# Odd weights' differences for gates, queries and keys made in the odd stage, and five units of output weights loaded inside the branch

## The chip, the cores and the metric

The kernel runs on one core of one Trainium2 chip. The metric is the device time of one execution in microseconds (us); lower is better. The engines are named as in the profile: PE (TensorE, matmuls), PEld (its weight loads), DVE (VectorE), ACT (ScalarE), POOL (GpSimd) and SP (SyncE, which only issues transfers here). POOL and ACT issue transfers too. Every engine works through its own list of instructions in the order that was fixed when the program was compiled.

## The reference, cut to what matters

A decoder of two layers, for one prompt of 2048 rows and for 64 sample rows (8 sequences of 8), model width 1024, all in float32.

```python
# layer 0 (even): pooling mixer and differential attention behind one projection
pu, pg, q, k, v, ag = split(x @ w_in_even)          # 1024 -> 3072
a   = softmax(q1 k1) - lam * softmax(q2 k2)         # 4 heads, causal
mix = concat([pool(pu) * silu(pg), rms_norm(a @ v) * silu(ag)])
y   = layer_norm(alpha * x + mix @ w_out_even)
# layer 1 (odd): gated linear attention, 4 heads, key 128, value 256
q, k, v, g = split(y @ w_in_odd)                    # 1024 -> 3072
log_a = log_sigmoid((y @ w_ga) @ w_gb + b_g) / 16
o, state = gla(q, k, v, log_a, state0)              # chunked scan
out = layer_norm(alpha * y + (rms_norm(o) * silu(g)) @ w_out_odd)
```

## The kernel before, in words

**Products.** A float32 product is made of three passes over a high and a low part (lines 51 to 53: high by high, low by high, high by low). Whatever PE multiplies is therefore split first: a copy that rounds to the high part (line 40 on ACT, 42 on POOL, 44 on DVE) and a subtraction for the low part (line 45). Weights come in units of 512 KB: a load by SP into one of two raw tiles (`wr`, line 375), then the split into one of four places.

**Fast products.** Both input projections are cut into groups of 1024 output columns: 0, 1, 2. For most groups the halves of rows, inner dimension and columns make a 2 by 2 block product, which `fast` computes with seven products instead of eight. It needs sums of the input's blocks (`s1` to `s4`) and, for each group, four differences of the weights' quarters (`t1` to `t4`). The class `WParts` makes those differences and keeps them in DRAM, in one of two ways:

- `make` works on pieces of 128 by 256: four loads, four subtractions (lines 301 to 304), four stores, all transfers issued by POOL (lines 351 and 353). One set of four tiles (pool `comb`) serves all pieces, eight pieces to a group.
- `make_wide` works on pieces of 4 by 128 by 512: one load (line 335; the first two of a call are issued by ACT, the others by POOL), the same four subtractions at twice the width, four stores by POOL (line 339). Two tiles take turns, four pieces to a group.

**Order of the even stage.** `project_even` runs groups 0, 1, 2 for the first 1024 rows and then for the second. Its local `run` advances a generator `parts` by one piece every so many steps. `parts` makes the even weights' own differences (groups 1 and 2 wide, group 0 narrow; tiles `pn` and `pmb`), and then the odd weights' differences for all three groups, narrow, in the order 1, 2, 0. In the profile these last are the tiles `rmb` and the DRAM tensor `rt`. `comb` is closed when the projection ends, and the pools that attention opens next take over that memory: among them `arp`, with the tiles `oq` (attention's results), `sga` (gates) and `sq`.

**Attention.** Heads 0 to 3, each over 16 blocks of 128 rows, `t` from 0. A block has scores (`sc`, lines 1016 and 1017), exponentials (`e`, line 1036), the difference of the two softmaxes (line 1045), transposes (`tp`, line 1068), products with the values (`po`, line 1061, one PSUM bank) and the copy of `po` into `oq` (line 1088, ACT). `weave` deals out filling work beside it by estimated cost: beside head 0 the first half of the output projection (`out_pool`, tiles `zp` on PE, `zh` and `zl` on POOL, 17 blocks of rows); beside head 1 the sample's attention (`Sample`, tiles `sk`, `ssc` and others), whose pool opens when `out_pool`'s memory is free; beside heads 2 and 3 the second half of the output projection with the norm.

**Order of the odd stage.** `project_odd` runs, for the first 1024 rows, group 0 with all eight products (`plain_rows`, which needs no differences), then group 1 and group 2 with `fast`; for the second 1024 rows groups 0, 1 and 2 with `fast`. Its local `run` advances a second generator beside the products: gates and the sums `s1` to `s4` of the input's blocks (`X.sums`). `s4` is used by the last of the seven products of `fast`.

**The branch.** After the projection the kernel loads the units `k` of the odd output weights (`w1_out`, eight in all, unit 0 earlier), reads one flag into a register and takes one of two branches, each of which runs the chunked scan `Gla.run`. Inside, `fill(i)` computes chunk `i` (`mix`: tiles `go` and `gsp`, state `S`), and `out(i)` multiplies its result by the eight units (`gz`). Nothing is moved across the branch.

The scheduler that fixes each engine's order simulates the program at compile time; the order in which the code states the work is its priority, so a piece stated early can run late.

Of the kernel before, what the change touches and what calls it, by code (L numbers as in the profile page):

```python
# [12 lines left out]
F32 = mybir.dt.float32  # L13
# [68 lines left out]
def places(wp):  # L82
    def f(i):
        return tuple(wp.tile([128, 1024], F32R, tag=f"w{z}", name=f"w{z}{i}") for z in "hl")
    return f
# [98 lines left out]
def fast(nc, X, w, fm, bank, qbank, room, sink, order=ORDER, scale=lambda j: 1.0, side=None):  # L184

    ps, t = {}, {}

    def open_(m, j):  # L190
        c = FIRST.get(m)
        if c:
            ps[c, j] = (qbank if c == "q" else bank)(f"f{m}_{j}")

    def mul(m, j, wm, k):
        p, a = ps[CHAIN[m], j], PARTS[m][0]
        js = slice(128 * j, 128 * j + 128)
        xs = [(lambda _, z=z: z[a][:, k, :] if fm else z[a][:, k, js]) for z in (X.hi, X.lo)]
        ws = [(lambda _, z=z: wm[z](k)[:, js] if fm else wm[z](k)) for z in range(2)]
        l, r = (ws, xs) if fm else (xs, ws)  # L200
        mm3(nc, p, *l, *r, 1, first=(m in FIRST and k == 0), last=(k == 3), skip_group_check=True)

    def done(m, j):
        p = ps[CHAIN[m], j]
        if m in (1, 6, 7):
            t[m, j] = room({1: "t", 6: "u", 7: "v"}[m], j)
            nc.scalar.activation(t[m, j], p, AF.Copy, scale=scale(j) if m == 1 else 1.0)
        elif m == 4:
            sink("21", j, p)
        else:  # L210
            o = t[{2: 1, 5: 7, 3: 6}[m], j]
            if m == 2 and scale(j) != 1.0:
                nc.vector.scalar_tensor_tensor(out=o, in0=p, scalar=scale(j), in1=o, op0=ALU.mult, op1=ALU.add)
            else:
                nc.vector.tensor_tensor(out=o, in0=p, in1=o, op=ALU.add)
            sink({2: "11", 5: "22", 3: "12"}[m], j, o)

    for m in order:
        wm = w(PARTS[m][1])
        if side:  # L220
            side(m, wm, True)
        for j in range(4):
            open_(m, j)
        for u in (0, 2):
            for j in range(4):
                for k in (u, u + 1):
                    mul(m, j, wm, k)
                if u:
                    done(m, j)
                    yield m, j  # L230
        if side:
            side(m, wm, False)
# [232 lines left out]
def project_even(tc, d, P, P2, W, slot, psf):  # L465


    nc = tc.nc
    xr, banks = ExitStack(), ExitStack()
    with ExitStack() as own:  # L470
# [72 lines left out]
        def all_parts():  # L543
            yield from P.make_wide(wide, (1, 2), X.last)
            yield from P.make(comb, (0,))

            P2.last = P.last
            yield from P2.make(comb, (1, 2, 0))

        parts = all_parts()  # L550

# [761 lines left out]
class Odd:  # L1313
# [34 lines left out]
    def run(self):  # L1348
        tc, d, ctx = self.tc, self.d, self.ctx
        nc = tc.nc  # L1350
        self.steep = self.pool(ctx, "p1s", 1).tile([1, 32], I32, name="steep")[:, 0:1]
        cst = self.pool(self.p1, "p1c", 1)
        tu = self.pool(self.p1, "p1t", 4)
        last = project_odd(tc, d, self, cst, tu)
        early = None
        for m, j in last:
            if (m, j) == (7, 3):

                self.xq.close()
                G = Gla(tc, d, self.ident, self.raw, self.pool(ctx, "gl", 1, side="right"))  # L1360
                early = self.early(G, self.pool(ctx, "gw0", 1, side="right"))
            elif early:
                next(early, None)
        for _ in early:
            pass
        self.p1.close()
        self.fill_banks.close()
        gw = places(self.pool(ctx, "gw", 3, side="right"))
        for k in range(1, 8):
            self.out_weights(G, k, gw if k > 4 else self.place)  # L1370
        G.buf["s"] = [self.raw.tile([128, 1024], F32, tag="raw", name=f"gs_{i}") for i in range(2)]
        r = nc.values_load(self.steep[0:1, 0:1], min_val=0, max_val=1)
        with tc.If(r < 1) as c:
            G.run(True)
        with c.Else():
            weights_inside(tc, d)
            G.run(False)
# [23 lines left out]
def plain_rows(X, nc, w, bank, sink):  # L1401

    for f in "12":
        wm = {i: w("b" + i + f) for i in "12"}
        for z in "12":
            ps = {}
            for i in "12":
                a = "a" + z + i
                for u in (0, 2):
                    for j in range(4):  # L1410
                        js = slice(128 * j, 128 * j + 128)
                        if j not in ps:
                            ps[j] = bank(f"f{z}{f}_{j}")
                        for k in (u, u + 1):
                            mm3(nc, ps[j], lambda _: wm[i][0](k)[:, js], lambda _: wm[i][1](k)[:, js],
                                lambda _: X.hi[a][:, k, :], lambda _: X.lo[a][:, k, :], 1,
                                first=(i == "1" and k == 0), last=(i == "2" and k == 3), skip_group_check=True)
                        if i == "2" and u:
                            sink(z + f, j, ps[j])
                        if j % 2:  # L1420
                            yield


def project_odd(tc, d, O, cst, tu):
# [92 lines left out]
    def queries_keys(h, given):  # L1517

        def sink(which, j, ap):
            t0 = 1024 * h + 512 * (which[0] == "2")  # L1520
            q = which[1] == "1"
            if not given or which == "21":
                e = slot(f"qe{h}{which}_{j}")
                nc.scalar.activation(e, ap, AF.Copy, scale=128 ** -0.5 if q else 1.0)
                ap = e
            nc.gpsimd.dma_start(d["q1" if q else "k1"][j, :, t0:t0 + 512], ap)
        return sink

    def values(h):
        def sink(which, j, ap):  # L1530
            t0 = 1024 * h + 512 * (which[0] == "2") + 128 * j
            if which == "21":
                e = slot(f"ve{h}_{j}")
                nc.scalar.activation(e, ap, AF.Copy)
                ap = e
            nc.gpsimd.dma_start(d["v1"][t0:t0 + 128, 512 * (which[1] == "2"):][:, :512], ap)
        return sink
# [40 lines left out]
            return cst.tile([128, 512], F32, tag="se", name=n)  # L1578
        return SampleSide(nc, x_s, qbank, place_, slot, done, name)

    def run(gen, then=(), wait=4):

        then = iter(then)
        for i, _ in enumerate(gen):
            if later:
                later.pop(0)()
            if i >= wait:
                next(then, None)

    def weights(g):  # L1590
        return P.loader(W, g)
# [5 lines left out]
    def first_parts():  # L1597
        yield from islice(sums, 8)
        ga, _ = gate_weights(0, False)
        for z in "12":  # L1600
            yield from gates(f"0{z}", 512 * (z == "2"), 512,
                             [t for i in "12" for k in range(4) for t in both(f"a{z}{i}", ga, k, 4 * (i == "2"))])

        yield from ("",) * 2
        for x in islice(sums, 4):
            yield x
# [1 line left out]
    def first_weights(x):  # L1608
        return O.first.pop(x) if x in O.first else weights(0)(x)

    run(plain_rows(X, nc, first_weights, bank, queries_keys(0, False)), first_parts(), wait=8)
    O.few.close()
    O.ev = O.pool(O.p1, "p1e", 8)
    run(fast(nc, X, weights(1), False, bank, qbank, place, values(0)), sums)
    nw = norm_weights(0)

    def next_parts():
# [84 lines left out]
class Gla:  # L1702
# [103 lines left out]
    def run_in(self, ctx, fast):  # L1806
# [31 lines left out]
        def prepare(i):  # L1838
            r = R[i]
            if i > 1:  # L1840
                yield from self.inside(i, 1, fast, bank)
            if i:
                self.split_v = self.two("v", r, "v1", "act")
            if i or not fast:
                self.two("a", r, "att", "dve")
            if i:
                r["qs"] = tuple(wk.tile([128, 4, 128], F32R, tag=f"q{z}", name=f"gq{z}{i}") for z in "hl")
                split(nc, r["q"], *r["qs"], "act")
# [173 lines left out]
        def fill(i):  # L2022
            yield from mix(i)
            if i:
                scale(i)
            else:

                yield from prepare(1)
                with tc.issue_after(self.split_v[0].ins), tc.issue_after(self.split_v[1].ins):
                    scale(0)  # L2030
            for _ in range(3):
                x = next(side, None)
                if x is not None:
                    yield x
            if 0 < i < 15:
                yield from prepare(i + 1)
            if i < 14:
                load(i + 2, first + ("v1",))
# [360 lines left out]
```

## Time and profile before

| | |
|---|---|
| three runs | 2235.43, 2237.23 and 3998.26 us, median 2237.23 |
| profiled execution | 2234.13 us, of which the span 2232.3 us |
| granted PE clock, mean | 0.962 of full speed |
| PE busy | 2042.4 us, 91% of the span, 10769 matmuls |
| DVE, ACT, POOL busy | 1525.8, 976.7 and 918.9 us |
| bytes moved | 405.67 MB, mean 182 GB/s |

The profile is of one execution and all its times are in us from the span's start, unless marked ns. "Busy" leaves out the issuing of transfers on SP, but for POOL the transfers' issue is counted. A row of waits reads: engine, tile, line, what ended the wait, total, times, longest. A row of the timeline reads: start, duration, engine, line, operation, written tile from read tile, shape, count, and in brackets the idle time just before it with what ended it. A row of stretches reads: start and end, length, busy time with the number of instructions in brackets for each engine, granted PE clock, share of the DMA engines, GB/s.

### The profile page before, as it was taken

How to read it: one execution, taken by the hardware profiler on the slowest of the kernel's cores; microseconds unless marked ns; L12 is line 12 of the kernel's file. 1: busy time of each engine (PE TensorE's matmuls, PEld its weight loads, DVE VectorE, ACT ScalarE, POOL GpSimd, SP SyncE). 2: the span in 40 equal slices, each digit the busy share in tenths (PEclk: the TensorE clock that was granted, in tenths of full speed). 3: DMA queues.
4: the chain of work that ended last, by engine and by line, in shares of the span. 5: the costliest groups of instructions: out<-in, count | busy, mean ns of one | idle time of the engine just before them, and what ended most of it. 6: DMA issues, size and time to landing. Idle time of an engine off the chain costs nothing. (4 is left out here: it accounts for less than half of the span.)

```text
span 2232.3 us, 31671 instructions
## 1 busy us (share of the span) xinstructions
PE 2042.4 (91%) x10769; PEld 1658.7 (74%) x10769; DVE 1525.8 (68%) x2905; ACT 976.7 (44%) x1809; POOL 918.9 (41%) x1257
## 2 busy tenths in 40 slices
PE   8999998989689999779888989999999896999987
PEld 7778786867557677667777768888887675877876
DVE  7697757757735676688676756736734558789994
ACT  4244342435302565465555533535527653333341
POOL 2445535346576334277463321122211122465654
PEclk9999999998899999899998999999999997999999
DMA  8877877469876778343232243456643457445522
GB/s 294 276 235 249 280 235 233 147 165 279 262 265 200 230 244 258 119 119 116 93 119 68 86 144 114 165 199 202 200 149 114 160 175 245 147 160 185 164 100 73
DMA packets 211294, 405.67 MB, mean 182 GB/s; under 512 B 30530, under 2 KB 107714, under 8 KB 211122
## 3 DMA queue, kind: packets, MB, share of 16 engines
q1 hardware_dynamic: 139490, 231.43, 34.2%
q0 software_dynamic: 52192, 160.59, 20.3%
q10 hardware_dynamic: 19440, 11.54, 1.7%
q8 instruction: 87, 1.43, 0.3%
q14 instruction: 85, 0.70, 0.1%
HBM read 275.90 MB, written 127.55 MB: 181 GB/s over the span
## 5 line engine op out<-in xcount | busy, mean ns | idle before, releaser
L1036 ACT ACTIVATE e<-sc,nm 128x896 f32<-128x896 f32 (+11 forms) x192 | 164.7, 863 | 95.0 <-DVE nm L1034 50.8
L1016 PE MATMUL sc<-kst,qh 128*128 128x512 f32 (+9 forms) x352 | 140.6, 402 | 45.1 <-ACT e L1036 44.9
L45 DVE TENSOR_TENSOR wk<-wr,wk 128x1024 fp32r<-128x1024 f32 x82 | 100.1, 1223 | 109.8 <-ACT wk L40 109.7
L1021 DVE TENSOR_REDUCE nm<-sc 128x1 f32<-128x768 f32 (+7 forms) x160 | 156.4, 990 | 24.7 <-PE sc L1017 16.0
L45 DVE TENSOR_TENSOR wl<-wr,wh 128x1024 fp32r<-128x1024 f32 (+1 forms) x93 | 110.5, 1191 | 82.1 <-ACT wh L40 69.6
L1061 PE MATMUL po<-vt,aT 128*128 128x128 f32 x1088 | 154.1, 284 | 1.9 <-ACT aT L1073 1.4
L40 ACT ACTIVATE wh<-wr 128x1024 fp32r<-128x1024 f32 (+1 forms) x86 | 89.1, 1038 | 150.3 <-PE f L52 62.2
L1061 PEld LDWEIGHTS po<-vt,aT 128*128 128x128 f32 x1088 | 140.1, 199 | 8.4 <-ACT aT L1073 2.3
L40 ACT ACTIVATE wk<-wr 128x1024 fp32r<-128x1024 f32 x78 | 82.2, 1057 | 123.4 <-PE f L53 95.5
L1017 PE MATMUL sc<-kst,ql 128*128 128x512 f32 (+9 forms) x352 | 126.6, 362 | 0.0
L1073 ACT ACTIVATE aT<-tp 128x512 f32<-128x512 f32 (+3 forms) x160 | 85.3, 533 | 88.3 <-PE tp L1068 87.4
L1016 PEld LDWEIGHTS sc<-kst,qh 128*128 128x128 f32 x352 | 71.3, 203 | 67.5 <-ACT e L1036 54.4
L1068 PE MATMUL tp<-ident,e 128*128 128x128 f32 x544 | 94.6, 292 | 17.4 <-ACT aT L1073 12.8
L1045 DVE SCALAR_TENSOR_TENSOR e<-e,c,e 128x128 f32<-128x128 f32 (+15 forms) x64 | 94.5, 1477 | 1.2
L1068 PEld LDWEIGHTS tp<-ident,e 128*128 128x128 f32 x544 | 66.5, 149 | 31.3 <-ACT aT L1073 18.0
L353 POOL DMA_DIRECT2D rt<-rmb x96 | 52.5, 549 | 75.9 <-DVE rmb L301 24.8
L1088 ACT ACTIVATE oq<-po 128x128 f32<-128x128 f32 x64 | 17.7, 276 | 146.3 <-DMA rt<-rmb 72.7
L1017 PEld LDWEIGHTS sc<-kst,ql 128*128 128x128 f32 x352 | 71.7, 204 | 3.3
L1092 POOL TENSOR_SCALAR s1q<-s 128x1 f32<-128x1 f32 x64 | 15.7, 248 | 132.8 <-DVE s L1039 103.6
L1039 DVE TENSOR_TENSOR s<-s 128x1 f32<-128x1 f32 x64 | 24.4, 381 | 66.1 <-ACT e L1036 65.7
L51 PE MATMUL zp<-wh,zh 128*128 128x512 f32 x128 | 54.9, 430 | 12.1 <-DVE zx L1188 5.8
L351 POOL DMA_DIRECT2D rmb<-in_w_q x96 | 52.7, 550 | 20.5 <-DMA rt<-rmb 15.8
(860 smaller groups left out, 6755.8 us busy)
## 6 DMA issues: line engine op xcount, KB each, us to landing
wr<-in_w_q SPq DMA_DIRECT2D x75, 512.0 KB
wr<-pt SPq DMA_DIRECT2D x40, 512.0 KB
wr<-rt SPq DMA_DIRECT2D x40, 512.0 KB
sk<-in_cachek SPq DMA_DIRECT2D x64, 256.0 KB
sv<-in_cachev SPq DMA_DIRECT2D x64, 256.0 KB
rmb<-in_w_q POOLq DMA_DIRECT2D x96, 128.0 KB, 4.2
rt<-rmb POOLq DMA_DIRECT2D x96, 128.0 KB, 3.9
pt<-pn POOLq DMA_DIRECT2D x32, 256.0 KB, 7.1
```

The costliest lines, as they stand in the source:

```text
L40: h = nc.scalar.activation(hi, raw, AF.Copy)
L45: return h, (lo_eng or nc.vector).tensor_tensor(out=lo, in0=raw, in1=hi, op=ALU.subtract)
L51: nc.tensor.matmul(ps, lh(k), rh(k), start=(first and k == 0), stop=False, **kw)
L351: nc.gpsimd.dma_start(b[-1], self.at(g, x)[:, c:c + n])
L1016: nc.tensor.matmul(o, qh[:, c, qs], kst[:, ks], start=True, stop=False)
L1017: nc.tensor.matmul(o, ql[:, c, qs], kst[:, ks], start=False, stop=k < npc - 1)
L1021: nc.vector.tensor_reduce(out=nm[:, c, i:i + 1], in_=p[:, :, :w], op=ALU.max, axis=AX.XY, negate=True)
L1036: nc.scalar.activation(o, p, AF.Exp, bias=nm[:, m, 0:1], accum_out=s[:, m, i if npc > 1 else 0:][:, :1])
L1045: nc.vector.scalar_tensor_tensor(out=es[0][:, :nk], in0=es[1][:, :nk], scalar=c2, in1=es[0][:, :nk], op0=ALU.mult, op1=ALU.add)
L1061: nc.tensor.matmul(po, s[:, 128 * j:128 * j + 128], vt[:, k0 + j, :], start=(k0 + j == 0), stop=(k0 + j == n - 1))
L1068: nc.tensor.transpose(p[:, 128 * j:128 * j + 128], a[:, 128 * (k0 + j):128 * (k0 + j) + 128], self.ident)
L1073: nc.scalar.activation(s[:, :128 * g], p[:, :128 * g], AF.Copy)
```

## The change

The even stage makes the odd weights' differences for group 1 only. Those for groups 2 and 0 are made in the odd stage, in wide pieces: six during its first run (group 0, first rows) and two during the next (group 1). Their two tiles are the memory in which `s4` is made afterwards, so `s4`'s sums start at step 20 of the second run instead of step 4. The first two loads are issued by ACT, in an order behind the last split of the input's first blocks, the other six by POOL. Of the output weights, units 1 and 2 are still loaded ahead of the branch; for units 3 to 7 only the places are taken there, and the loads and splits stand inside the branch, in `fill(0)` behind `prepare(1)`. There the raw tiles are the two that the branch also uses for the sample's states.

```diff
@@ project_even, all_parts @@
             P2.last = P.last
-            yield from P2.make(comb, (1, 2, 0))
+            yield from P2.make(comb, (1,))
@@ Odd.run @@
+        for k in range(1, 3):
+            self.out_weights(G, k, self.place)
         gw = places(self.pool(ctx, "gw", 3, side="right"))
-        for k in range(1, 8):
-            self.out_weights(G, k, gw if k > 4 else self.place)
+        for k in range(3, 8):
+            G.w.append((gw if k > 4 else self.place)(300 + k))
@@ project_odd @@
-    def run(gen, then=(), wait=4):
+    def run(gen, then=(), wait=4, every=0):
         then = iter(then)
         for i, _ in enumerate(gen):
             if later:
                 later.pop(0)()
+            if every and i % every == 1:
+                next(parts, None)
             if i >= wait:
                 next(then, None)
+
+    def wide(name):
+        wide.turn = 1 - wide.turn
+        return left[2].tile([128, 4, 512], F32, tag="hl"[wide.turn], name=name)
+
+    wide.turn = 1
+    parts = P.make_wide(wide, (2, 0), X.last)
@@
-    run(plain_rows(X, nc, first_weights, bank, queries_keys(0, False)), first_parts(), wait=8)
+    run(plain_rows(X, nc, first_weights, bank, queries_keys(0, False)), first_parts(), wait=8, every=6)
@@
-    run(fast(nc, X, weights(1), False, bank, qbank, place, values(0)), sums)
+    run(fast(nc, X, weights(1), False, bank, qbank, place, values(0)), sums, wait=20, every=5)
@@ Gla.run_in, fill @@
                 yield from prepare(1)
+                for k in range(3, 8):
+                    x = self.get("s")
+                    nc.sync.dma_start(x, d["w1_out"][k])
+                    split(nc, x, *w[k], "act" if k % 2 else "dve")
                 with tc.issue_after(self.split_v[0].ins), tc.issue_after(self.split_v[1].ins):
                     scale(0)
```

## The prediction

> **What bounds the kernel now.** I read the page's first rows, then a view of stretches, then the waits and the timeline in the stretch that looked worst.
>
> ```profile
> span 2232.3 us, 31671 instructions
> PE 2042.4 (91%) x10769; PEld 1658.7 (74%) x10769; DVE 1525.8 (68%) x2905; ACT 976.7 (44%) x1809; POOL 918.9 (41%) x1257
> ```
>
> PE is the busiest engine, and the change takes no matmul away. What it can win are the 190 us in which PE idles and the time in which its clock is low. The stretches say where those are.
>
> ```profile
> 228.00:580.00 352.00, 326.97 (x1399) 261.81 (x1397) 238.60 (x401) 138.97 (x222) 176.31 (x307) 0.96 0.73 228
> 580.00:680.00 100.00, 75.33 (x272) 54.68 (x272) 42.59 (x74) 7.81 (x13) 67.45 (x103) 0.86 0.82 257
> 680.00:740.00 60.00, 57.73 (x333) 49.03 (x334) 38.22 (x91) 21.81 (x54) 37.49 (x60) 1.00 0.55 168
> 740.00:810.00 70.00, 66.89 (x646) 50.72 (x647) 48.14 (x125) 42.39 (x104) 21.80 (x38) 1.00 0.80 256
> 810.00:900.00 90.00, 87.65 (x892) 66.76 (x894) 62.71 (x184) 52.51 (x133) 36.41 (x58) 0.98 0.77 245
> 900.00:967.00 67.00, 46.63 (x296) 38.21 (x296) 46.15 (x88) 33.34 (x68) 20.97 (x26) 0.87 0.37 115
> 1320.00:1420.00 100.00, 100.00 (x451) 81.71 (x450) 57.92 (x92) 39.87 (x63) 12.00 (x22) 1.00 0.36 116
> 1420.00:1700.00 280.00, 280.00 (x1249) 231.35 (x1248) 158.28 (x219) 119.40 (x172) 50.78 (x93) 1.00 0.54 180
> ```
>
> The odd stage, 1320 to 1700, is full: 451 wide matmuls in 100 us are 0.222 us each. Between 580 and 680 PE ran only 272 in 100 us. Nearly all are `zp`, work meant to fill in beside attention:
>
> ```profile
> 580.00:680.00 100.00, 73.87 (x267) 53.55 (x267) 15.07 (x22) 0.86 0.82 257
> ```
>
> At 0.222 us the 267 are 59 us of work, so 40 us are lost, part as idle time, part in the clock of 0.86. Why attention stood still is told by ACT's timeline and by the row of tile `rmb`, the narrow pieces of the odd weights' differences:
>
> ```profile
> 607.59 1.15 ACT L967 ACTIVATE kst<-kr 128x512 fp32r<-128x512 f32 x2 [4.98 <-DMA kr<-k]
> 681.40 0.28 ACT L1088 ACTIVATE oq<-po 128x128 f32<-128x128 f32 x1 [72.66 <-DMA rt<-rmb]
> ```
> ```profile
> L351 POOL DMA_DIRECT2D rmb<-in_w_q x96: 536/541/1032, 228.7 to 673.8; - x96
> L353 POOL DMA_DIRECT2D rt<-rmb x96: 539/542/606, 242.6 to 678.9; - x96
> L301 DVE TENSOR_TENSOR rmb<-rmb,rmb x24: 402/420/1492, 241.9 to 675.1; 128x256 f32<-128x256 f32 x24
> ```
>
> `oq` lies where the four `comb` tiles lay. Its first write waits for the last store of the 24 pieces, 72.66 us; with one PSUM bank for `po`, no second product with values can start before. Line 1045, once per head and block, shows the hole (blocks 8 and 9 of head 0, its last, and head 1's last):
>
> ```profile
> 582.20 2.27 DVE L1045 SCALAR_TENSOR_TENSOR e<-e,c,e 128x1024 f32<-128x1024 f32 x1
> 701.40 1.42 DVE L1045 SCALAR_TENSOR_TENSOR e<-e,c,e 128x1152 f32<-128x1152 f32 x1
> 803.79 2.35 DVE L1045 SCALAR_TENSOR_TENSOR e<-e,c,e 128x2048 f32<-128x2048 f32 x1
> 962.02 2.34 DVE L1045 SCALAR_TENSOR_TENSOR e<-e,c,e 128x2048 f32<-128x2048 f32 x1
> ```
>
> From 701.40 to 803.79 seven blocks took 14.6 us each; from 582.20 to 701.40 one took 119. The hole costs twice. `zp` was used up during it, so the sample's work, here its scores,
>
> ```profile
> L2126 PE MATMUL ssc<-sk,sqs x128: 589/593/617, 743.1 to 874.1; 128*32 128x512 f32 x128
> ```
>
> began under head 0's tail and ran out early; head 1's last blocks, 900 to 967, then had nothing beside them: 20 us idle and 13% of 47, 6 us, in the clock, 26 together.
>
> **The change, part by part.** *Fewer narrow pieces (16 of 24 go).* Removed: 128 issues on POOL by 0.54, 69 us; 64 subtractions by 0.42, 27 us of DVE; 16 x 8 x 128 KB, 16.8 MB. The eight pieces that stay are, by the count of subtractions of `rmb`, those before 400:
>
> ```profile
> 228.00:400.00 172.00, 13.39 (x32) 36.45 (x67) 0.98 0.74 247
> ```
>
> That is 180 us before `oq` wants the memory. Then nothing that I see holds `oq`: the memory's other tenants (gate weights, the pooling tiles) end with the projection, whose place `zp` takes from 580 on.
>
> The gain, from 580 to 967: 40 us lost in the hole, 26 in the tail, and 2.3 + 3.1 + 2.4 idle between, 74 of 387; 313 us of full work. With attention and filling together PE was busy 57.73 + 66.89 of 130 us, 95.9% at clock 1.00. 313 / 0.959 = 326, which is 61 us less: the upper end. The lower end is the hole alone at that rate, 40 - 59 x 0.043 = 37, less 4 for the smaller filling later, 33. Attention's own pace sets no later limit: head 0's eight blocks left at 14.6 from 582 end at 699, and head 1 took 962.02 - 803.79 = 158, so 857, ahead of 967 - 61 = 906. I take **50**: the sample's pool opens when `zp` is done, which would now be at the end of head 0, so most of the tail is covered, not all.
>
> *Other relief before 580.* DVE works in order, and here it stood behind a narrow load, then PE behind DVE:
>
> ```profile
> 500.62 0.42 DVE L302 TENSOR_TENSOR rmb<-rmb,rmb 128x256 f32<-128x256 f32 x1 [8.80 <-DMA rmb<-in_w_q]
> ```
> ```profile
> 502.51 0.42 PE L51 MATMUL pl<-dh,lin 128*128 128x64 f32 x1 [4.31 <-ACT dh L40]
> 503.98 0.42 PE L52 MATMUL pl<-dl,lin 128*128 128x64 f32 x1 [1.05 <-DVE dl L45]
> 505.00 0.63 PE L52 MATMUL f<-wl,xs3h 128*128 128x512 f32 x1
> 505.43 0.63 PE L53 MATMUL f<-wh,xs3l 128*128 128x512 f32 x1
> ```
>
> 4.31 + 1.05 idle, then matmuls start 0.43 apart instead of 0.222 for some 4 us, 2 more: 7.4. Bounds 0 (another load takes the place) and 12 (half of the 25 us that PE idles from 228 to 580); I take **6**.
>
> *Wide pieces in the odd stage (8 added).* The even stage's own wide pieces, tile `pn`, are the nearest rows:
>
> ```profile
> L301 DVE TENSOR_TENSOR pn<-pn x8: 679/692/693, 28.4 to 102.1; 128x512 f32<-128x512 f32 x8
> L339 POOL DMA_DIRECT2D pt<-pn x32: 539/542/719, 29.4 to 114.4; - x32
> L335 POOL DMA_DIRECT2D pn<-in_w_q x6: 748/762/784, 37.1 to 95.4; - x6
> L335 ACTq DMA_DIRECT2D pn<-in_w_q x2: 431/476/521, 21.6 to 22.0; - x2
> ```
> ```profile
> DVE pn L301 <- DMA pn<-in_w_q: 18.2, 4, 7.6
> PE f L51 <- ACT wh L40: 3.5, 3, 1.6
> PE f L53 <- DVE wl L45: 3.0, 2, 1.6
> ```
>
> Added: 32 subtractions by 0.69, 22 us of DVE, 17 of them in the first run, where DVE is busy 57.92 of 100; 32 stores by 0.54 and six loads by 0.76, 22 us of POOL, where it is busy 63 of 380; two issues on ACT, 1 us; 16.8 MB, 126 GB/s over the first run's 100 us beside 116. All fits beside a full PE. What can reach PE is order: DVE stands behind each wide load, up to 7.6 us, and behind it in its list wait the low parts of PE's weights and the gates' arithmetic; on POOL a load waits for the stores two pieces earlier, and behind it the stores of queries, keys and gates, for whose slots ACT's evictions wait. The cover is the four weight places: a unit serves 24 matmuls, 5.3 us, so a freed place is needed again after 16 us, more than 7.6 plus 2.8 of subtractions. `s4`, made here some 40 us ahead of its first product:
>
> ```profile
> 1433.14 2.49 DVE L141 TENSOR_TENSOR ys4r<-ya12h,ya21h 128x512 f32<-128x512 f32 x4
> ```
> ```profile
> L51 PE MATMUL f<-wk,ys4h x64: 387/389/398, 1484.1 to 1854.0; 128*128 128x512 f32 x64
> ```
>
> is now stated four steps, some 6 us, ahead; 16 steps of 0.62 are 10 us, and PE needs the first half at once. If they were not brought forward PE would wait 3 us and run slow for 4 more, 5 in all. The price lies between 0 and 6.5 + 5, 12: the waits on weights in the even stage's first 300 us (3.5 + 3.0) with eight such pieces, plus `s4`. I take **4**.
>
> The Trainium skill ("Perfetto Trace Analysis", DMA Optimizations) speaks against wide pieces here: where the DMA engines are mostly idle, it holds, smaller transfers let some work start sooner. The stretch 1320 to 1420 has them 0.36 busy, yet the longest DVE wait was 8.80 behind a narrow piece and 7.6 behind a wide one, so the trace does not bear it out. By that rule the odd term would be at worst the 18.2 / 4 of each wait eight times, 36 us, and the sum 2211.
>
> *Output weights inside the branch.*
>
> ```profile
> PE gsp L51 <- DVE S L1881: 12.4, 2, 11.8
> ```
> ```profile
> 1865.00 1.23 DVE L45 TENSOR_TENSOR wl<-wr,wh 128x1024 fp32r<-128x1024 f32 x1 [2.48 <-ACT wh L40]
> 1867.27 0.69 DVE L44 CAST wh<-wr 128x1024 fp32r<-128x1024 f32 x1 [1.05 <-DMA wr<-in_w_out]
> 1870.88 0.68 DVE L44 CAST Sh<-gsp 128x512 fp32r<-128x512 f32 x1
> ```
>
> PE waits 11.8 us for the first chunk's state while DVE still splits units 6 and 7 ahead of the branch, idle 3.5 us of it. Moved behind `prepare(1)`, the splits (five by 1.23, two by 0.69, 7.5 us of DVE) no longer stand ahead of the state, but ahead of `scale(0)` and the first `gz`, and their five loads now go through two raw tiles on SP behind the branch's first loads. DVE's work is the same; what surely goes is its idle 3.5. Ends: a gain of 8 (the state 8 us sooner, all used) and a loss of 3 (`gz` waits for unit 7). I take **3**.
>
> Sum on the profiled execution's 2234.1 (span plus 1.8): 2234.1 - 50 - 6 + 4 - 3 = 2179. The median of the runs is 3 us higher; I forecast 2180.
>
> **The rivals.**
>
> *A: the hole only changes owner.* Another tenant of `oq`'s memory, or the remaining pieces run as late as their place in the list allows, holds it as long. For: pieces stated by step 24 of the projection did run at 679. Against: the row names `rt<-rmb` alone, and the first eight ran by 400. Then only the other terms count: 2234 - 6 + 4 - 3 = 2229.
>
> *B: the hole closes but the tail stays.* The sample again runs ahead of head 1. Then 33 instead of 50: 2196.
>
> *C: all ends are good.* 61, 10, 0 and 6: 2157.
>
> *D: the wide pieces stall the odd stage, slower than before.* Place: first and second run. Each of eight pieces holds DVE 7.6 us, its weights come late, PE idles as long and runs at half clock for 4 us, 2 more: 8 x 9.6 = 77, against 59 gained: 2252. It decides from 59 / 8 = 7.4 us a piece. Against: 16 us of cover, and 6.5 us in all for eight pieces in the even stage.
>
> *E: no change in time.* Since PE is busy 91% and its work is untouched, everything moved is off the path: 2234. The Trainium skill ("Perfetto Trace Analysis", Identifying the Most-Contended Engine) says to optimise the engine with the highest occupancy first, which here would be PE; its next section, on strategy, would look at the gaps of that engine, and the stretches above agree with the second, 25 idle and a clock of 0.86 in one hundred.
>
> **How the numbers follow.** Forecast 0.45 (own range 2166 to 2196); A 0.10, B 0.20, C 0.15, D 0.05, E 0.05. A change under 2% can't be told from none here; faster by that means below 2192. The forecast lies there nine times in ten (0.41), C always (0.15), B in a third (0.06): faster 0.62. The rest is within 2%, but for 0.02 beyond D. The range holds the forecast, B and C with their spread: 2152 to 2212.
>
> **What the new profile would show.** The wait of `oq` on `rt<-rmb` gone, line 1045 without a hole after 582, head 0 ending near 745 and head 1 near 915, the odd stage beginning 50 to 60 us sooner. `rmb` 32 loads instead of 96. In the odd stage PE at 100% beside `pn`-like pieces; a `gsp` wait well below 11.8. It is wrong if line 1088 still waits tens of us for a transfer, if 900 to 967 repeats at head 1's end, or if the first odd runs show PE waiting for low parts of weights.

## The result, and the profile after

The changed kernel takes 2159.69 us (median of four, 2155.88 to 2162.52) against 2236.40 for the kernel before (median of three): a ratio of 0.966, with a 95% interval of 0.964 to 0.968. It is 77 us faster, where the forecast was 55 to 57. The three runs of the kernel before that are used lie between 2235 and 2237 us; a fourth, at 3998, is left out. The profiled execution took 2162.52 us, 71.6 less than the profiled one of before.

The head of the page of the changed kernel: the same number of matmuls, in a shorter span.

```profile
span 2160.7 us, 31464 instructions
...
PE 2014.4 (93%) x10769; PEld 1643.7 (76%) x10769; DVE 1527.5 (71%) x2872; ACT 979.8 (45%) x1812; POOL 885.1 (41%) x1167
```

The stretches of the changed kernel that answer to those from 580 to 967. Together they hold nearly the same work (2473 matmuls against 2439) in 325 us instead of 387, but not row by row, since attention and filling now run side by side; the columns are those of the tables above (length, busy time and count of PE, PEld, DVE, ACT, POOL, then clock, share of the transfers, GB/s).

```profile
562.00:662.00 100.00, 98.69 (x546) 83.65 (x545) 70.02 (x154) 41.31 (x90) 50.29 (x73) 0.98 0.67 205
662.00:720.00 58.00, 58.00 (x321) 48.53 (x320) 39.64 (x60) 21.75 (x44) 31.98 (x40) 1.00 0.54 162
720.00:780.00 60.00, 55.60 (x531) 43.86 (x529) 43.48 (x135) 35.84 (x95) 30.35 (x57) 1.00 0.76 239
780.00:870.00 90.00, 85.80 (x913) 65.44 (x912) 58.56 (x153) 49.55 (x119) 24.25 (x41) 0.98 0.87 279
870.00:887.00 17.00, 14.69 (x162) 12.16 (x160) 12.55 (x25) 11.49 (x27) 12.32 (x14) 1.00 0.35 96
```

Where PE ran 272 matmuls in the 100 us from 580, it now runs 546 from 562. The last 67 us, in which PE was busy 46.63 us at clock 0.87, have an answer in the 67 us up to 887: there it is busy 61.73 at 0.97. The narrow pieces' stores (tile view) and ACT's first copy into `oq` (timeline) in the changed kernel:

```profile
L353 POOL DMA_DIRECT2D rt<-rmb x32: 542/547/606, 242.7 to 391.5; - x32
```
```profile
559.07 0.28 ACT L1088 ACTIVATE oq<-po 128x128 f32<-128x128 f32 x1
```

No wait stands behind it. Line 1045 in DVE's timeline: head 0's blocks 0, 7, 8 and 15 and head 1's block 15, and below them block 0 in the kernel before.

```profile
529.89 1.36 DVE L1045 SCALAR_TENSOR_TENSOR e<-e,c,e 128x128 f32<-128x128 f32 x1
...
574.73 1.38 DVE L1045 SCALAR_TENSOR_TENSOR e<-e,c,e 128x1024 f32<-128x1024 f32 x1
588.15 1.42 DVE L1045 SCALAR_TENSOR_TENSOR e<-e,c,e 128x1152 f32<-128x1152 f32 x1
...
703.47 2.35 DVE L1045 SCALAR_TENSOR_TENSOR e<-e,c,e 128x2048 f32<-128x2048 f32 x1
...
882.85 2.56 DVE L1045 SCALAR_TENSOR_TENSOR e<-e,c,e 128x2048 f32<-128x2048 f32 x1
```
```profile
547.40 1.46 DVE L1045 SCALAR_TENSOR_TENSOR e<-e,c,e 128x128 f32<-128x128 f32 x1
```

From block 7 to block 8 it is 13.4 us instead of 119 (the prediction counts these two from one, as 8 and 9). Two gains can be told apart here: attention begins earlier, and it takes less time. How much falls to each depends on where the line between them is drawn. The first block starts 17.5 us earlier, and from there to head 1's last block it is 353.0 us instead of 414.6, 61.6 less. But block 1 now follows the first after 14.5 us instead of 5.6:

```profile
544.35 1.80 DVE L1045 SCALAR_TENSOR_TENSOR e<-e,c,e 128x256 f32<-128x256 f32 x1
```
```profile
553.02 0.48 DVE L1045 SCALAR_TENSOR_TENSOR e<-e,c,e 128x256 f32<-128x256 f32 x1
```

By block 7 (574.73 against 582.20) the lead is down to 7.5 us, and from there to head 1's last block it is 308.1 us instead of 379.8, 71.7 less.

Read so, the kernel falls into five stretches, which the rest of the text uses: to the first block; from there to head 1's last block; to the last first-pass product of `op` with row tile `oh` (line 51); to the last product of `s4` (`ys4h`, line 51); and to the end of the span. In us, from one trace each (the changed kernel from two):

| kernel | first block | to head 1's last | to last `op` | to last `s4` | to the end |
|---|---|---|---|---|---|
| before | 547.4 | 414.6 | 368.9 | 523.1 | 378.3 |
| changed | 529.9 | 353.0 | 369.8 | 528.6 | 379.5 |
| changed, again | 532.4 | 349.4 | 367.3 | 527.9 | 378.7 |
| eight pieces held back | 527.1 | 411.4 | 369.1 | 523.1 | 374.9 |
| sixteen pieces | 551.9 | 343.6 | 373.6 | 523.5 | 377.2 |
| 24 pieces, room of their own | 551.3 | 364.4 | 390.4 | 520.2 | 376.7 |
| eight pieces, room of their own | 535.7 | 365.8 | 379.0 | 529.1 | 376.4 |
| no wide pieces | 533.5 | 348.7 | 371.7 | 523.7 | 374.1 |
| branch part undone | 532.7 | 349.8 | 367.6 | 529.9 | 375.3 |
| branch part alone | 549.1 | 417.5 | 368.3 | 525.2 | 368.4 |

### The profile page after: what moved, and what is told of

It reads as the page before. It is cut to its first block, busy times and chain, and to the rows that moved or that the text cites. A ratio compares the mean times of both kernels' runs of the same rounds, so it can differ in the third digit from the quotient of the medians.

```text
span 2160.7 us, 31464 instructions
## 1 busy us (share of the span) xinstructions
PE 2014.4 (93%) x10769; PEld 1643.7 (76%) x10769; DVE 1527.5 (71%) x2872; ACT 979.8 (45%) x1812; POOL 885.1 (41%) x1167
## 5 line engine op out<-in xcount | busy, mean ns | idle before, releaser
L1021 DVE TENSOR_REDUCE nm<-sc 128x1 f32<-128x768 f32 (+7 forms) x160 | 156.8, 991 | 28.9 <-PE sc L1017 16.6
L45 DVE TENSOR_TENSOR wk<-wr,wk 128x1024 fp32r<-128x1024 f32 x80 | 98.1, 1229 | 95.9 <-ACT wk L40 95.6
L1016 PE MATMUL sc<-kst,qh 128*128 128x512 f32 (+9 forms) x352 | 136.2, 390 | 28.0 <-ACT e L1036 27.2
L1068 PE MATMUL tp<-ident,e 128*128 128x128 f32 x544 | 92.0, 284 | 13.4 <-ACT aT L1073 12.1
L53 PE MATMUL op<-wh,ol 128*128 128x512 f32 x128 | 52.3, 409 | 5.1 <-DVE ol L1232 5.1
L53 PE MATMUL gz<-wh,gml 128*128 128x512 f32 x128 | 51.5, 404 | 3.2 <-DVE gml L45 3.1
L51 PE MATMUL gz<-wh,gmh 128*128 128x512 f32 x128 | 52.7, 413 | 1.9 <-ACT gmh L40 1.8
L51 PE MATMUL op<-wh,oh 128*128 128x512 f32 x128 | 53.1, 415 | 1.2 <-ACT oh L1231 1.1
```

The source lines that it names most:

```text
L45: return h, (lo_eng or nc.vector).tensor_tensor(out=lo, in0=raw, in1=hi, op=ALU.subtract)
L51: nc.tensor.matmul(ps, lh(k), rh(k), start=(first and k == 0), stop=False, **kw)
L53: nc.tensor.matmul(ps, ll(k), rh(k), start=False, stop=(last and k == n - 1), **kw)
L1016: nc.tensor.matmul(o, qh[:, c, qs], kst[:, ks], start=True, stop=False)
L1021: nc.vector.tensor_reduce(out=nm[:, c, i:i + 1], in_=p[:, :, :w], op=ALU.max, axis=AX.XY, negate=True)
L1068: nc.tensor.transpose(p[:, 128 * j:128 * j + 128], a[:, 128 * (k0 + j):128 * (k0 + j) + 128], self.ident)
```

## The experiments

### The hole: is it the memory, or the pieces' work?

**The same eight pieces, held back.** Their transfers are put behind the gates' stores of the even projection's last group in POOL's list; nothing is added or left out.

```diff
-            yield from P2.make(comb, (1,))
+            late.extend([P2.make(comb, (1,))])
...
-            nc.gpsimd.dma_start(d["sg0"][t0:t0 + n, :], e)
+            state["gst"] = nc.gpsimd.dma_start(d["sg0"][t0:t0 + n, :], e)
...
+            if m in (4, 5):
+                P2.last = state["gst"]
+                next(late[0])
             yield m, j
...
```

> The changed kernel, but the transfers of its eight narrow pieces stand behind the gates' stores of the even projection's last group in POOL's list, so they cannot run before some 525; the work is the same. In the two runs that only stated them later they ran at 230 to 393 all the same. At 11 to 17 us a piece they end between 615 and 660. Theory (the wait on the memory of `oq` makes the hole): line 1088 waits 50 to 100 us on the last store of `rmb`, head 1 ends 30 to 60 us later than in the changed kernel, 2190 to 2215. Rival (16 pieces' work that is gone made the gain, the wait is a symptom): 2155 to 2172.

Measured: 2203.4 us, 0.985 of the kernel before (0.983 to 0.988), against 2159.27 for the changed kernel in another comparison: 44 us slower with the same work. The pieces' stores, ACT's timeline and DVE's timeline of this run (line 1045 is line 1050 here):

```profile
L353 POOL DMA_DIRECT2D rt<-rmb x32: 539/540/603, 522.8 to 651.4; - x32
```
```profile
653.77 0.28 ACT L1093 ACTIVATE oq<-po 128x128 f32<-128x128 f32 x1 [64.29 <-DMA rt<-rmb]
```
```profile
570.23 1.28 DVE L1050 SCALAR_TENSOR_TENSOR e<-e,c,e 128x1024 f32<-128x1024 f32 x1
669.65 1.42 DVE L1050 SCALAR_TENSOR_TENSOR e<-e,c,e 128x1152 f32<-128x1152 f32 x1
...
938.42 2.34 DVE L1050 SCALAR_TENSOR_TENSOR e<-e,c,e 128x2048 f32<-128x2048 f32 x1
```

A wait of 64.29 us on the last store is back, with the hole at the same block (99 us from block 7 to 8) and 411 us to head 1's last block. Against the changed kernel's 349 to 353 that is some 60 us. The rival falls. The whole kernel loses 44, as the other stretches are a few us shorter in this trace. The pieces' work now lies beside attention too, so this run alone doesn't put all 60 down to the wait; the runs with a room of their own, below, bear on that.

**Only stated later.** Two runs tried this first without the tie to POOL's list: one stated the eight pieces 16 turns later, by the line below, the other during the last group, by the diff above without its lines on `gst`.

```diff
+            yield from (None,) * 16
             yield from P2.make(comb, (1,))
```

> The changed kernel, but the eight narrow pieces that stay are stated 16 pieces later, where the last third of the 24 stood. Theory (what counts is when the last piece leaves the memory of `oq`, not how many pieces there are): the wait of line 1088 on the last store of `rmb` returns with 50 to 75 us, and with it the hole and the tail of head 1; the even stage keeps some of its relief; 2205 to 2230. Rival (the gain is the 16 pieces' work that is no longer done in the even stage): the time stays within 10 us of 2159.7.

> The changed kernel, but its eight narrow pieces are stated during the last group of the even projection, one at each step of its fifth and sixth product, so they cannot run before some 520. At 17 us a piece (16 pieces took from 400 to 679 in the kernel before) they end near 650. Theory (the memory of `oq`): line 1088 waits 50 to 90 us on the last store of `rmb`, the hole and the tail are back, 2190 to 2215, while the even stage gains a few us more. Rival (the gain came only from the work of 16 pieces that is gone): 2155 to 2170.

Measured: 2156.3 and 2154.73 us, no change. The stores of the second:

```profile
L353 POOL DMA_DIRECT2D rt<-rmb x32: 539/544/606, 243.6 to 393.2; - x32
```

Stated during the last group, they still ran from 243 on, so neither run tested the theory. They show that in this program the place in the source does not hold an independent transfer back; a tie to an instruction on its own engine does.

**Sixteen narrow pieces**, groups 1 and 2, with four wide ones left for the odd stage.

```diff
-            yield from P2.make(comb, (1,))
+            yield from P2.make(comb, (1, 2))
...
-    parts = P.make_wide(wide, (2, 0), X.last)
+    parts = P.make_wide(wide, (0,), X.last)
```

> The changed kernel with 16 narrow pieces in the even stage (odd groups 1 and 2) and only group 0's four wide pieces in the odd stage. Theory (a threshold): the 16 end near 530, ahead of the first write of `oq` at 559, so no hole; eight more pieces cost the even stage about half of its 10.7 us and the odd stage gets some 2 back: 2160 to 2168. Rival (in proportion): the gain of 77 is shared by the 16 pieces, so eight of them cost 38: 2198.

Measured: 2169.26 us, 0.969 (0.965 to 0.973). The stores and two blocks:

```profile
L353 POOL DMA_DIRECT2D rt<-rmb x64: 539/542/603, 242.0 to 546.4; - x64
```
```profile
551.90 1.45 DVE L1045 SCALAR_TENSOR_TENSOR e<-e,c,e 128x128 f32<-128x128 f32 x1
...
895.54 2.33 DVE L1045 SCALAR_TENSOR_TENSOR e<-e,c,e 128x2048 f32<-128x2048 f32 x1
```

The last store is issued at 546, ahead of attention's first copy, and attention has no hole (343.6 us). But its first block is as late as with 24 pieces. So the gain comes in two steps and not in proportion: the last eight pieces cost 69 us, most of it through the memory (attention's stretch is 71 us shorter), the eight before them 10, by their work ahead of attention: the last product of the even projection starts at 559.97, and at 549.70 in the changed kernel. The 10 are net of four wide pieces fewer in the odd stage. The threshold theory stands; its range, up to 2168, was a little low.

**A room of their own.** `comb` stands in memory that nothing else uses until head 0 is over, once in the kernel before with 24 pieces, once with the eight.

```diff
+        comb = left.enter_context(tc.tile_pool(name="p0m", bufs=1))
         raw = left.enter_context(tc.tile_pool(name="p0raw", bufs=2))
...
-        comb = own.enter_context(tc.tile_pool(name="p0m", bufs=1))
```

> The kernel before, with its 24 narrow pieces and all their work, but the four `comb` tiles stand in memory of their own that stays theirs until head 0 is over. Theory (the hole is the overlap of `oq` with `comb`, not the amount of work): the 72.66 us wait of line 1088 is gone, line 1045 shows no hole after 582, head 1's last block starts 55 to 70 us earlier than 962.02; the time is 2165 to 2185, worse than the changed kernel's 2159.7 only by the even stage's 10.7 us that the pieces still cost, less the odd stage's 4. Rival (the pieces' own load on DVE, POOL and the transfers held attention): the hole stays as line 1045 shows it, 2230 to 2240.

> As the run with the eight pieces last, but `comb` stands in memory of its own, so nothing waits for it. The difference between the two is the wait alone, at the same work. Theory: no wait of line 1088, 2160 to 2178, where what is above 2160 is the load of eight pieces beside attention (16 pieces beside it made head 1 end 21 us later, counted from the last even product). Rival (the pieces' work, not the memory, held attention): the same time as that run, within 10 us.

Measured: 2198.62 us, 0.982 (0.978 to 0.987), and 2180.47 us, 0.976 (0.974 to 0.978). With 24 pieces, the stores, ACT's first copy into `oq`, and the first and last block:

```profile
L353 POOL DMA_DIRECT2D rt<-rmb x96: 539/542/627, 246.3 to 723.3; - x96
```
```profile
569.12 0.28 ACT L1088 ACTIVATE oq<-po 128x128 f32<-128x128 f32 x1 [4.34 <-PE po L1061]
```

```profile
551.32 1.46 DVE L1045 SCALAR_TENSOR_TENSOR e<-e,c,e 128x128 f32<-128x128 f32 x1
...
915.70 2.35 DVE L1045 SCALAR_TENSOR_TENSOR e<-e,c,e 128x2048 f32<-128x2048 f32 x1
```

The wait is gone and attention takes 364 us instead of 415, though 24 pieces run until 723 beside it. That speaks for the memory again. Both times are above what was expected, because the room itself costs: with eight pieces, which ran at 233 to 397 as in the changed kernel, it makes the time 21 us longer (2180.47 against 2159.27 in one comparison). What the 4 KB displaced was not looked into, so neither run prices the wait by itself. The pair does better: with a room of their own, 24 pieces and eight leave attention's stretch the same (364.4 and 365.8 us), and the two kernels 18 us apart, where without it they are 77 apart. If the room costs both alike, which is not shown, the wait is worth the difference, some 59 us.

### The odd stage

> The changed kernel without the eight wide pieces: the odd weights' differences for groups 2 and 0 are left out (quarters are read in their place, by the same loads), and `s4` starts at step 4 of the second run as before. It prices the whole odd term. Theory from the two traces (the odd stage gave back 3.7 us of 76.5): 2154 to 2158 against 2159.7. Rival, the prediction's upper bound of 12 or more: 2148 or less. Second rival, the pieces are hidden wholly: 2159 to 2161.

```diff
-    parts = P.make_wide(wide, (2, 0), X.last)
+    parts = iter(())
...
-    run(fast(nc, X, weights(1), False, bank, qbank, place, values(0)), sums, wait=20, every=5)
+    run(fast(nc, X, weights(1), False, bank, qbank, place, values(0)), sums, wait=4, every=5)
...
-        return self.src[g, QUARTERS.index(x)] if x[0] == "b" else self.t[g][x]
+        return self.src[g, QUARTERS.index(x)] if x[0] == "b" else self.src[g, int(x[1]) - 1] \
+            if self.pre == "r" and g != 1 else self.t[g][x]
```

Measured: 2151.4 us, 0.963 (0.958 to 0.968). The time lies between the theory's range and the first rival's; the changed kernel's 0.967 (0.965 to 0.970) overlaps it, so the stretch has to say more. The last `s4` product comes 523.7 us after the last `op`, as in the kernel before (523.1), and 528.6 and 527.9 in the changed kernel. Windows of 50 us show where, first in the changed kernel, then in this one:

```profile
1300.00:1350.00 50.00, 46.47 (x202) 36.84 (x200) 35.90 (x52) 22.64 (x36) 19.82 (x36) 1.00 0.90 321
1350.00:1400.00 50.00, 49.27 (x211) 40.69 (x212) 30.71 (x44) 20.51 (x30) 8.91 (x17) 0.97 0.56 181
```
```profile
1300.00:1350.00 50.00, 50.00 (x220) 40.71 (x219) 32.92 (x48) 26.33 (x43) 8.59 (x16) 1.00 0.40 133
1350.00:1400.00 50.00, 50.00 (x222) 41.39 (x222) 27.76 (x37) 21.01 (x30) 7.03 (x13) 1.00 0.44 150
```

With the pieces 413 matmuls, without them 442: 29 at 0.222 us are 6. The waits of PE in the changed kernel name the low part of a weight:

```profile
PE f L52 <- DVE wk L45: 5.9, 3, 3.9
```

The row of the kernel before:

```profile
PE f L52 <- DVE wk L45: 1.9, 1, 1.9
```

The weight's high part, its low part and the matmul that waited, in the changed kernel:

```profile
1341.35 1.04 ACT L40 ACTIVATE wk<-wr 128x1024 fp32r<-128x1024 f32 x1
```
```profile
1349.46 1.22 DVE L45 TENSOR_TENSOR wk<-wr,wk 128x1024 fp32r<-128x1024 f32 x1
```
```profile
1350.73 0.79 PE L52 MATMUL f<-wk,ya12h 128*128 128x512 f32 x1 [3.89 <-DVE wk L45]
```

From 1342.4 on, DVE could have made the low part; it first ran the gates' arithmetic and five subtractions of wide pieces, and waited 1.0 us for a load of theirs. So the low part stood behind them in DVE's list, as the forecast said it could. It happened once, not eight times. And it is no fixed price of the pieces: in two of the kernels that only order the narrow pieces otherwise (eight held back, 523.1 us, and stated during the last group, 523.5 us) the eight wide pieces run in the same place, no wait on `wk` is longer than 2.0 us, and the stretch is as short as without them. In the other traces with eight wide pieces it is 528 to 533.

The Trainium skill ("Perfetto Trace Analysis", DMA Optimizations) says that splitting transfers may let some start sooner where the DMA engines are generally idle. No run here has both widths in one place, so that was not tested.

**Pieces stated every ninth step** instead of every sixth.

```diff
-    run(plain_rows(X, nc, first_weights, bank, queries_keys(0, False)), first_parts(), wait=8, every=6)
+    run(plain_rows(X, nc, first_weights, bank, queries_keys(0, False)), first_parts(), wait=8, every=9)
```

> The changed kernel with the wide pieces stated at every ninth step of the odd stage's first run instead of every sixth. In the changed kernel all eight ran from 1265 to 1358, the transfers were 0.90 busy from 1300 to 1350, and PE lost 6 us there. Theory (the pieces crowd each other): spread over some 140 us, the loss is gone, 2151 to 2156. Rival (the pieces are free to run as soon as their tiles are, whatever step states them): the same place and the same time as the changed kernel, within 3 us. Second rival: `s4` now waits for the later pieces and its first product stalls, 2160 to 2168.

Measured: 2158.14 us, 0.967 (0.965 to 0.969). The wide pieces' stores in this run, then in the changed kernel:

```profile
L339 POOL DMA_DIRECT2D rt<-rn x32: 539/540/557, 1275.4 to 1358.2; - x32
```
```profile
L339 POOL DMA_DIRECT2D rt<-rn x32: 542/542/560, 1274.5 to 1358.3; - x32
```

The first rival is right: same place, same time. Whether spreading them would win the 4 to 5 us of this stretch was thus not tried.

### The branch

> The changed kernel with the output weights loaded ahead of the branch again, all eight units; the differences stay in the odd stage. Theory from the two traces (the first `gz` came 6.4 us sooner after the projection, and all of it was given back inside the branch, where DVE is busy 35 to 39 of 40 us): 2157 to 2162, the same as the changed kernel's 2159.7, and the first `gz` some 6 us later after the projection's last product. Rival, the prediction's term: the branch part brings 3 (at most 8), so without it 2163 to 2168.

> The kernel before with the branch part alone: five units of output weights loaded and split inside the branch. Theory (given back inside the branch): 2234 to 2239 against 2236.8. Rival, the prediction's term: 2229 to 2234.

The edit is the change's part in `Odd.run` and `fill`, taken back in the first run (below) and made alone in the second.

```diff
-        for k in range(1, 3):
-            self.out_weights(G, k, self.place)
...
-        for k in range(3, 8):
-            G.w.append((gw if k > 4 else self.place)(300 + k))
+        for k in range(1, 8):
+            self.out_weights(G, k, gw if k > 4 else self.place)
...
-                for k in range(3, 8):
-                    x = self.get("s")
-                    nc.sync.dma_start(x, d["w1_out"][k])
-                    split(nc, x, *w[k], "act" if k % 2 else "dve")
```

Measured: 2157.18 us, 0.966 (0.964 to 0.969), without the branch part; 2230.24 us with it alone, 0.9975 of the kernel before (0.9960 to 0.9989), 2 to 9 us faster. The first lies in its theory's range; the second lies in its rival's, so there the theory failed. The first `gz` of before, changed, and branch part alone (one row of each kernel's tile view):

```profile
L51 PE MATMUL gz<-wh,gmh x128: 390/393/775, 1887.3 to 2220.2; 128*128 128x512 f32 x128
```
```profile
L51 PE MATMUL gz<-wh,gmh x128: 388/393/775, 1808.1 to 2148.3; 128*128 128x512 f32 x128
```
```profile
L51 PE MATMUL gz<-wh,gmh x128: 390/393/555, 1885.4 to 2218.1; 128*128 128x512 f32 x128
```

Counted from the last `s4` product, `gz` starts after 33.3 us before, 26.9 in the changed kernel and 25.3 with the branch part alone. So 6 to 8 us are won at the start. In the changed kernel's trace the span then ends 379.5 us after that product against 378.3: all is given back. With the branch part alone the stretch is 368.4. Over the traces in the table it lies between 368 and 380 with the branch part and 375 to 378 without, so a trace cannot settle a term this small. One timed pair shows a gain of 2 to 9, the other none that it can tell.

**High parts on ACT, low parts on POOL** for the five units, to take 7.5 us from DVE in the branch.

```diff
-                    split(nc, x, *w[k], "act" if k % 2 else "dve")
+                    split(nc, x, *w[k], "act", nc.gpsimd)
```

> The changed kernel, but inside the branch the five units' high parts are all made by ACT and their low parts by POOL, so that DVE has 5 x 1.22 + 2 x 0.69 = 7.5 us less in the branch. Theory (DVE is what gives the first 6 us back): most of the 7.5 is won, 2152 to 2156. Rival (the loss is the start of the chunks, or the order of `gz` behind the weights): 2159 to 2162; if POOL's subtractions come too late for the first `gz`, which then starts later than 27 us after the projection's last product, 2162 to 2168.

Measured: 2173.78 us, 0.973 (0.971 to 0.976), slower than the changed kernel and worse than every theory said. The last stretch grew to 389.6 us, and the first `gz` was not late (26.3 us). POOL's timeline:

```profile
1825.49 2.38 POOL L45 TENSOR_TENSOR wl<-gs,wh 128x1024 fp32r<-128x1024 f32 x1 [3.18 <-ACT wh L40]
```

A low part takes POOL 2.38 us where the row of before has DVE at 1.23, and POOL's list also holds the decayed queries and keys that every chunk needs. The run didn't do what it was made for: DVE is busy 312.6 us in the last stretch here and in the changed kernel alike, with seven instructions fewer, because others took longer (line 1783 0.96 us in the mean instead of 0.32). Why they did was not looked into. So whether DVE limits the branch stays open, and why so much was lost is only argued.

## Why the prediction was right, and where a size was off

**The hole, -50 with bounds 33 to 61: right mechanism, too small, and beyond its bound.** The wait of `oq` on the last store held attention; holding eight pieces back made the hole again, for some 60 us. The forecast's sum parts the kernel at 580, and block 7 stands there in the kernel before (582.20). From block 7 to head 1's last block the changed kernel takes 71.7 us less (73.6 by its second trace). PE alone in this part, in the kernel before and the changed one (start and end, length, busy time and count, clock, share of the transfers, GB/s):

```profile
582.20:962.00 379.80, 331.30 (x2415) 0.94 0.68 215
```
```profile
574.70:882.80 308.10, 298.27 (x2373) 0.99 0.69 216
```

Two steps failed. The first is the choice of 50 on the ground that "most of the tail is covered, not all". The sample's scores ran

```profile
L2141 PE MATMUL ssc<-sk,sqs x128: 589/593/617, 739.7 to 849.2; 128*32 128x512 f32 x128
```

after head 0's end at 703, not under its tail, and its other products lasted to 877, six us short of head 1's last block. The tail was covered nearly whole: PE idles 5.3 of the last 67 us instead of 20.4. Head 0's last block started at 703 and head 1's at 883, where 745 and 915 had been named. The second is the upper bound. PE's busy share is as assumed there, 96.8% at clock 0.99 for 95.9% at 1.00, but less work was left. The products with values that PE had run by block 7, before and after:

```profile
0.00:582.20 582.20, 0.46 (x2) 0.97 0.75 242
```
```profile
0.00:574.70 574.70, 6.45 (x38) 0.98 0.73 233
```

These 36 products, 6 us, had been held by the same wait already ahead of 580, where the forecast's window begins: with eight pieces held back there are again two by block 7, with sixteen pieces 42. The other 5 us beyond the bound were not traced.

**Other relief, -6 with bounds 0 to 12: right by the forecast's own cut.** Block 7 came 7.5 us sooner (6.6 in the second trace), and the last product of the even projection started at 549.70 instead of 556.25. Only the first block came 17.5 us sooner, and most of that was lost again by block 7. From 400 to 540, in stretches of the kernel before, the changed one, the one with sixteen pieces and the one with eight held back:

```profile
400.00:540.00 140.00, 127.25 (x533) 102.42 (x532) 93.26 (x168) 65.25 (x99) 65.95 (x107) 0.94 0.67 187
```
```profile
400.00:540.00 140.00, 133.43 (x585) 107.11 (x584) 90.08 (x150) 73.05 (x113) 43.32 (x59) 0.99 0.59 153
```
```profile
400.00:540.00 140.00, 124.35 (x520) 99.08 (x519) 87.44 (x164) 61.30 (x95) 61.22 (x102) 0.94 0.65 176
```
```profile
400.00:540.00 140.00, 133.21 (x583) 107.14 (x581) 83.43 (x137) 69.25 (x112) 45.77 (x62) 0.99 0.59 161
```

Where narrow pieces run in this stretch PE gets 520 to 533 matmuls at a clock of 0.94, elsewhere 583 to 585 at 0.99. Of the 52 more in the changed kernel 38 are even products (tile `f`, 507 against 469), 8.4 us. The stall that the forecast had priced is gone, and another on the same tiles: PE waited 9.2 us for `dh` and `dl` in this stretch and now waits 1.2. The clock, which the forecast put at a small part, gave about as much as the idle time, 12.8 us before and 6.6 now. What the POOL time (66 to 43 us) had to do with it was not traced.

**Odd stage, +4 with bounds 0 to 12: right, but not a fixed price.** It was 5 (528.6 and 527.9 against 523.1), through the weights' low parts, in one place, and nothing in the two traces named above. `s4` cost nothing that shows.

**Branch, -3 with bounds -8 to +3: not contradicted.** `gsp` waits 6.9 us at most instead of 11.8, and `gz` starts 6 us sooner; the profiled executions then differ by +1, the two timed pairs by 0 and -6.

Summed with the cut at block 7: -7.5, -71.7, +0.9, +5.5, +1.2, which is -71.6, the span's whole difference. The 16.6 us between the forecast of -55 and this are 21.7 from the hole and 1.5 from the other relief, less 4.2 in the branch, 1.5 in the odd stage and 0.9 in heads 2 and 3. The measured 2159.7 lies outside the forecast's own range of 2166 to 2196, and inside the wide one because that was drawn to hold rival C, all ends good (2157), which was nearest. It was nearest partly by luck: the hole went beyond C's 61, and the odd stage and the branch fell short of C's ends. A falls with the first copy at 559, B with the covered tail, D with 5 us instead of 77, E with the result.

## What to carry to other kernels

A tile that is only scratch can hold up whatever is placed over it later: look for a long wait of a copy or a store on a transfer that has nothing to do with its data, and price the hole together with the filling work that runs out because of it. Making the last use early enough is worth all of it, making it earlier still is worth only the work that moves out of the busy stretch. And before an experiment on order is believed, look in its trace whether the order changed.

## What was not expected

Eight wide pieces beside a full PE brought the transfers to 0.90 busy and 321 GB/s from 1300 to 1350, and PE idled 3.5 us in those 50. And the lower clock went with the narrow pieces: 0.94 from 400 to 540 in the two kernels where they ran all through it, 0.99 in the two where they did not, and up to there these four programs differ in the pieces alone.
